# Routing written in another order, later loads in the first mixer, second blocks of 32 slots, one more weight buffer, and products that nothing reads

## The chip, the cores and the metric

One core of a Trainium2 chip runs the whole program in one launch. The metric is the device time of that core in microseconds (us); of several executions the median is taken.

## What is computed

256 tokens of width 1024 pass through two transformer blocks, all in fp32. The reference, cut to what matters here:

```python
# first block
h = x
z = rms_norm(h) @ w_in                       # q, k, v, u: 4 x 512 columns
h = h + concat(diff_attention(q, k, v), pool_mixer(u)) @ w_out
xt = rms_norm(h); logits = xt @ w_router + b_router
top_vals, top_idx = lax.top_k(logits, 4); gates = softmax(top_vals)
# 32 experts: three weights of 1024 x 1024 and three biases each
gt = minimum(x_e @ w_gate[e] + b_gate[e], 7); up = clip(x_e @ w_up[e] + b_up[e], -7, 7)
y_e = ((up + 1) * (gt * sigmoid(1.702 * gt))) @ w_down[e] + b_down[e]
h = h + sum_e gate_e * y_e
h = h + sigmoid(rms_norm(h) @ w_ple_gate) * rms_norm(p @ w_ple_proj)
# second block
x = x + mixer_2(rms_norm(x))                 # sliding window attention and a gated recurrence
x = x + hierarchical_moe(rms_norm(x))        # 4 groups of 8 experts, top 2, 1024 x 512 weights
```

With the reference's inputs the fullest expert of the first mixture gets 73 tokens, the next 64; in the second mixture no expert gets more than 26.

## The kernel before, in words

**Weights.** All large weights stream through SBUF in chunks of 1 MB (`wchunk`, 128 x 2048), which SyncE's queue (SP) loads in the order of use. A chunk goes into the first free buffer of some pools: 7 that stay for the whole kernel, and in the first mixture 4 + 6 more (`NX[False]`, pools `m1_xa` and `m1_xc`). SP takes its loads in order; one that waits for its buffer holds back all loads behind it. The products of the mixers run on split operands (`xh`, `xl` times `w_hi`, `w_lo`): ScalarE (ACT) writes `w_hi`, VectorE (DVE) writes `w_lo`, TensorE (PE) makes three matmuls of 128x512 per piece and token tile. Four such pairs (`AHEAD + 2`) are in flight.

**First mixer** (`attend_pool`, 0 to about 113 us). Four blocks of 512 columns of `w_in` (q, k, v, u), attention as a generator that is advanced between matmuls (`side`), the pool mixer (`bands`, `wpool`), then `w_out`, whose sums are added to the residual `h_res`. Two small tables for what follows are loaded at its start: the experts' biases (`bias_sb`, 786 KB, in two DMAs; ACT copies them, DVE subtracts a low part) and the routers' weights (`wr_sb`, 278 KB; DVE multiplies them by the norm's gains).

**Route** (`route`, once for each mixture). For each of the two token tiles t: turn `h_res` (PE transposes into `ts`, evacuated as `w_hi` by ACT and DVE), `logits`, `choose` (DVE: top k, one-hot `sel`), `keep` (`xth` on ACT, its low part `xtl` in two halves on DVE), `place` (PE products `po` of `sel` with triangular and constant matrices: a token's slot within its expert). `weights` makes the gates and, as int32, the counts `cnt`. Then the one-hots `P`, and the gather (`ga`: PE, 8 matmuls per bank) that brings the tokens of four (second mixture: eight) experts into `xg`. The order on each engine is as written (`manual_schedule`).

**Mixtures.** `all_experts` does 64 slots of an expert with 512 columns at a time: `gate(e+1)`, `down(e)`, `up(e+1)`. If an expert has more than 64 tokens, a second block of 64 slots (`extra`) is done at once, with the same weights still in their buffers. If one has more than the limit of `more` (128), its weights are loaded again. With these inputs the second block is needed once, for expert 0. `narrow_experts` does the second mixture: 32 slots of an expert, four products of 256 columns that lie on the four quarters of PE's rows.

Of the kernel before, what the change touches and what calls it, by code (L numbers as in the profile page):

```python
# [78 lines left out]
class Prog:  # L79
# [346 lines left out]
    def specs(self):  # L426
# [116 lines left out]
    def attend_pool(self, ph, xh, xl):  # L543

        nc, tc = self.nc, self.tc
        if True:
# [7 lines left out]
            wpool = sb.tile([128, 4, 128], F32, name="wpool")  # L554
# [55 lines left out]
            self.wr = self.cst.tile([128, 8, 68], F32, name="wr_sb")  # L610
            nc.sync.dma_start(self.wr, self.A["wr"])
            for g, a, b in ((PK_FFN, 0, 32), (PK_NORM2, 32, 68)):
                col = self.pk[:, g:g + 8].unsqueeze(2).to_broadcast([128, 8, b - a])
                self.tt(self.wr[:, :, a:b], self.wr[:, :, a:b], col, OP.mult)
# [19 lines left out]
            self.cp(self.bias, bias)  # L634
            low = self.bias[64:128]
            self.tt(low, bias[64:128], low, OP.subtract)
# [3 lines left out]
            for _ in side:  # L640
                pass
            return acc
# [153 lines left out]
    def mixer2(self):  # L796
        nc, tc = self.nc, self.tc
        with ExitStack() as ph:
# [7 lines left out]
            with tc.tile_pool(name="b_ple", bufs=2, reuse_waits="tile") as gp:  # L806
                ws = self.p_q
                self.pieces_begin(sp, 29, 0)
                self.norm_tr(self.h[:, 0], 0, xh, xl)
                ss = self.small.tile([128, 2, 2], F32, name="gss")  # L810
# [24 lines left out]
                for t in range(2):  # L835
                    for n in range(4):
                        for i in range(2):
                            self.lin_mm(ps[t], xh, xl, 2 * n + i, ws[n], i, t, n == 0 and i == 0, n == 3 and i == 1)
                        if t == 0 and n == 1:
                            self.norm_tr(self.h[:, 1], 1, xh, xl)  # L840
                            self.piece_emit()
                            stats()
                        if t == 0 and n == 3 or t and n < 2:
                            self.piece_emit()
                    gated(0)(t, ps[t])
# [374 lines left out]
    def route(self, ph, xh, xl, accs):  # L1220
# [17 lines left out]
        def turn(t):  # L1238
            x = r["xT"][t] = self.sp.tile([128, 8, 128], F32, name="w_hi", bufs=self.AHEAD + 2)
            for k4 in range(2):  # L1240
                ps = self.ps.tile([128, 4, 128], F32, name="ts", bufs=3)
                for k in range(4):
                    i = 4 * k4 + k
                    self.tr(ps[:, k], self.h[:, t, i * 128:(i + 1) * 128])
                if k4:
# [4 lines left out]
        def keep(t):  # L1250

# [3 lines left out]
            f = r["r"][:, t:t + 1]  # L1255
            self.cp(xth, xp, f)
            for i in range(2):
                at = (slice(None), slice(None), i) if k == 2 else (slice(None), i)
                self.stt(xtl[at], xp[at], f, xth[at], OP.mult, OP.subtract)
# [4 lines left out]
        def mid():  # L1264
            turn(0)

# [3 lines left out]
        def added(j):  # L1270
            add = self.res(j)

            def f(t, p):
                add(t, p)
                if t == 0:
                    squares(t, j)
                    if j:
                        factor(0)
                        keep(0)
            return f  # L1280

        with tc.manual_schedule():
# [88 lines left out]
    def one_hots(self, c, e0, ne, base, n=64):  # L1371

        P = self.scr.tile([128, 2, ne, n], FR, name="P" if ne > 1 else "PT2", bufs=2 if ne > 1 else 1)
# [4 lines left out]

    def gather(self, c, P):

        ne, n = P.shape[2:]
        xg = self.scr.tile([128, 8, ne, n], F32, name=f"xg{ne}", bufs=1)
        per = 512 // (ne * n)

        def banks():
            for k0 in range(0, 8, per):
                ps = self.bank("ga").rearrange("p (k e s) -> p k e s", k=per, e=ne)
# [15 lines left out]

    def gathered(self, c, P):
        xg, banks = self.gather(c, P)
# [21 lines left out]
    def slots(self, c, e, buf, base=0, n=64):  # L1427
# [6 lines left out]
        i = base // 32 if n == 64 else 8  # L1434
        slot = self.slot[:, i:i + 1]
        self.ts(PT, ps[:, 0], slot, OP.is_equal)
        room = self.scr.tile([128, 2, 128], F32, name="room", bufs=1)
# [20 lines left out]
    def act_fn(self, c, g, u, hd=None, room="act_s"):  # L1458

        nc, scr, W = self.nc, self.scr, c["W"]  # L1460
# [13 lines left out]
        return hd  # L1474

# [58 lines left out]
    def first_tokens(self, c):  # L1534

        P = self.one_hots(c, 0, *((8, 0, 32) if c["second"] else (4, 0)))
        xg, banks = self.gather(c, P)
# [3 lines left out]
    def bias_sel(self, c, e, eng=None):  # L1541
# [3 lines left out]
        sel = self.scr.tile([128, 2, 64], FR, name="bselx" if eng else "bsel", bufs=1 if eng else 2)  # L1545
# [26 lines left out]
    def all_experts(self, c):  # L1572
# [6 lines left out]
        def product(e, part, main, extra):  # L1579
# [3 lines left out]
            with tc.If(st["cnt", e] > 64):  # L1583
                extra(keep)
            self.w_done(4)

        def gate(e, sides=()):
# [4 lines left out]
            def extra(ws):  # L1592
                st["xx"] = self.gathered(c, self.one_hots(c, e, 1, 64))
                gx = self.linear_up(c, st["xx"], 0, ws, sel, self.bias[:, 0], self.bank("ga"))
                hx = st["hx", e] = self.scr.tile([128, c["W"]], F32, name="gx", bufs=2)
                self.cp(hx, gx)
# [3 lines left out]
        def up(e, room="act_s"):  # L1600
# [3 lines left out]
            def extra(ws):  # L1604
                ux = self.linear_up(c, st["xx"], 0, ws, sel, self.bias[:, 1], self.bank("tph"))
                self.act_fn(c, st["hx", e], ux, st["hx", e], room)
# [6 lines left out]
        def down(e, hT, sides):  # L1613
# [3 lines left out]
            def extra(ws):  # L1617
                PTx, gsx = self.slots(c, e, 2, 64)
                yx = self.linear_down(c, self.turn_h(c, st["hx", e], "act_x"), ws, sel, self.bank("ga"))
                for _ in self.combine(c, PTx, self.weigh(yx, gsx, ("act_x", "gxm"))):  # L1620
                    pass
# [6 lines left out]
        for e in range(32):  # L1628
# [7 lines left out]
            if e == 29:  # L1636
                self.w_keep = [self.xps["m1_xa"]] * 4
# [13 lines left out]
            if e == 30:  # L1651
                room = lambda: self.xps["m1_xa"].tile([128, 2048], F32, name="wchunk")
                self.pieces_begin(None, 2, 4, room)
# [111 lines left out]
    def more(self, c):  # L1765

        tc, most = self.tc, 32 if c["second"] else 128
# [52 lines left out]
    NX = {False: (4, 6), True: (4, 5, 3)}  # L1820
# [68 lines left out]
```

## Time and profile before

| what | value |
|---|---|
| three executions | 1806.77, 1803.26 and 1806.77 us |
| profiled execution | 1803.07 us, span in the trace 1801.2 us |
| PE, DVE, ACT busy | 87%, 38%, 21% of the span |
| DMA | 658.88 MB, 366 GB/s in the mean |
| first mixer, first route | 0 to 113 us, 113 to 128 us |
| first mixture | 128 to 1108 us |
| second mixer, second route | 1108 to 1317 us, 1317 to 1348 us |
| second mixture | 1348 to 1797 us |

The profiled execution lies 0.2% below the median, like the second of the three. Starts are in us from the beginning of the span. A busy PE also runs at one of two clocks: a granted clock of 1.0 is 2.4 GHz, 0.5 is 1.2 GHz. What ended an engine's idle time stands in brackets behind a row.

### The profile page before, as it was taken

What the parts mean: (1) busy time and instruction counts of PE and PEld (TensorE: products, weight loads), DVE (VectorE), ACT (ScalarE), POOL (GpSimd) and SP (SyncE); (2) the same over time, 40 slices, a digit from 0 to 9 for tenths busy, and PEclk for the clock granted to TensorE, in tenths of its full rate; (3) what the DMA queues carried; (4) which work ended last, traced back from release to release, by engine and by line L of the source; (5) the groups of instructions that cost most, each with busy time, mean ns of one, the idle gap of its engine ahead of it and who ended that gap; (6) DMA issues with size and microseconds to landing.
All of it is one profiled execution on the core that took longest, in us unless ns stands there. A gap on an engine that the chain in (4) does not pass through costs nothing. (4 is left out here: it accounts for less than half of the span.)

```text
span 1801.2 us, 24529 instructions
## 1 busy us (share of the span) xinstructions
PE 1566.4 (87%) x9887; PEld 763.6 (42%) x9887; DVE 678.2 (38%) x1389; ACT 373.6 (21%) x765; POOL 25.2 (1%) x61
## 2 busy tenths in 40 slices
PE   6989999999998988989899988999979777777776
PEld 5763333333332322323233324789965433433333
DVE  4851222222322222222132334878754333323234
ACT  5631010010100100101001023786632100100100
POOL 0000000000000000000000000000000000000000
PEclk9989999999999999999899999999989977979788
DMA  9374899999999999999999997533669999999997
GB/s 349 125 297 177 328 423 424 422 423 422 424 423 424 423 424 423 423 422 424 421 424 422 424 403 307 191 121 131 242 244 404 423 424 424 424 423 423 421 424 313
DMA packets 109979, 658.88 MB, mean 366 GB/s; under 512 B 10480, under 2 KB 12400, under 8 KB 36080
## 3 DMA queue, kind: packets, MB, share of 16 engines
q1 hardware_dynamic: 108944, 655.19, 89.0%
q8 instruction: 119, 1.95, 0.4%
q10 hardware_dynamic: 720, 0.79, 0.1%
q0 software_dynamic: 144, 0.52, 0.1%
q14 instruction: 52, 0.43, 0.1%
HBM read 655.41 MB, written 1.05 MB: 364 GB/s over the span
## 5 line engine op out<-in xcount | busy, mean ns | idle before, releaser
L94 DVE TENSOR_TENSOR h_res<-h_res,cmb 128x512 f32<-128x512 f32 x260 | 167.1, 684 | 320.4 <-PE cmb L85 320.4
L85 PE MATMUL u<-wchunk,xg 128*64 128x512 f32 x1024 | 236.3, 604 | 21.6 <-DMA wchunk<-in_w_up_dram 21.5
L85 PE MATMUL g<-wchunk,xg 128*64 128x512 f32 x1024 | 250.3, 611 | 0.0
L85 PE MATMUL y<-wchunk,act_s 128*64 128x512 f32 x1024 | 236.7, 600 | 6.1 <-DMA wchunk<-in_w_down_dram 6.1
L85 PE MATMUL gu<-wchunk,xg 128*32 128x256 f32 x2048 | 181.4, 462 | 67.5 <-DMA wchunk<-in_w_up_experts_dram 39.4
L85 PEld LDWEIGHTS u<-wchunk,xg 128*64 128x64 f32 x1024 | 68.4, 138 | 169.3 <-issue 113.7
L85 PEld LDWEIGHTS gu<-wchunk,xg 128*32 128x32 f32 x2048 | 74.8, 128 | 152.4 <-DMA wchunk<-in_w_up_experts_dram 55.4
L85 PEld LDWEIGHTS y<-wchunk,act_s 128*64 128x64 f32 x1024 | 66.7, 136 | 131.1 <-issue 106.5
L91 ACT ACTIVATE yh<-y,gs 128x512 fp32r<-128x512 f32 (+1 forms) x64 | 37.2, 581 | 394.1 <-PEq L1583 286.9
L102 DVE SCALAR_TENSOR_TENSOR yl<-y,gs,yh 128x512 fp32r<-128x512 f32 (+1 forms) x64 | 39.5, 617 | 196.6 <-ACT yh L91 196.5
L85 PEld LDWEIGHTS g<-wchunk,xg 128*64 128x64 f32 x1024 | 62.9, 137 | 106.5 <-issue 95.3
L85 PE MATMUL cmb<-yh,PT 32*128 32x256 f32 (+1 forms) x384 | 75.4, 460 | 31.6 <-DVE h_res L94 30.5
L91 ACT ACTIVATE act_s<-tph 128x256 f32<-128x256 f32 x32 | 12.3, 384 | 361.5 <-PE tph L88 361.5
L85 PE MATMUL lin<-w_hi,xh 128*128 128x512 f32 (+1 forms) x192 | 77.8, 405 | 10.4 <-ACT w_hi L91 8.9
L102 DVE SCALAR_TENSOR_TENSOR w_lo<-wchunk,pk_sb,w_hi 128x512 fp32r<-128x512 f32 (+1 forms) x120 | 83.3, 729 | 9.0 <-ACT w_hi L91 8.6
L85 PEld LDWEIGHTS cmb<-yh,PT 32*128 32x128 f32 (+1 forms) x384 | 33.1, 203 | 117.5 <-DVE h_res L94 64.5
L91 ACT ACTIVATE w_hi<-wchunk,pk_sb 128x512 fp32r<-128x512 f32 (+1 forms) x120 | 77.9, 699 | 16.7 <-PE lin L85 14.1
L98 DVE TENSOR_SCALAR act_h<-u 128x512 f32<-128x512 f32 x32 | 22.1, 692 | 156.3 <-PE u L85 156.3
L85 PE MATMUL lin<-w_lo,xh 128*128 128x512 f32 (+1 forms) x192 | 75.6, 394 | 5.6 <-DVE w_lo L102 4.7
L98 DVE TENSOR_SCALAR PT<-ga,cmain 128x256 fp32r<-128x256 f32 x65 | 31.0, 477 | 121.1 <-PE ga L85 121.1
L85 PE MATMUL lin<-w_hi,xl 128*128 128x512 f32 (+1 forms) x192 | 75.5, 393 | 0.5 <-DVE xl L125 0.5
L85 PE MATMUL y<-wchunk,hT 128*32 128x256 f32 x1024 | 65.0, 385 | 10.4 <-DMA wchunk<-in_w_down_experts_dram 9.7
(386 smaller groups left out, 1923.0 us busy)
## 6 DMA issues: line engine op xcount, KB each, us to landing
wchunk<-in_w_gate_dram SPq DMA_DIRECT2D x128, 1024.0 KB, 19.7
wchunk<-in_w_up_dram SPq DMA_DIRECT2D x128, 1024.0 KB, 19.7
wchunk<-in_w_down_dram SPq DMA_DIRECT2D x128, 1024.0 KB, 19.7
wchunk<-in_w_gate_experts_dram SPq DMA_DIRECT2D x64, 1024.0 KB, 19.7
wchunk<-in_w_up_experts_dram SPq DMA_DIRECT2D x64, 1024.0 KB, 19.7
wchunk<-in_w_down_experts_dram SPq DMA_DIRECT2D x64, 1024.0 KB, 19.7
wchunk<-in_w_in_dram SPq DMA_DIRECT2D x27, 1024.0 KB, 5.4
wchunk<-in_w_out_dram SPq DMA_DIRECT2D x8, 1024.0 KB, 5.1
```

Source lines behind the costliest of these rows:

```text
L85: self.nc.tensor.matmul(out, lhsT, rhs, start=start, stop=stop, skip_group_check=True)
L91: self.nc.scalar.activation(out=out, in_=in_, func=AF.Copy, scale=scale)
L94: self.nc.vector.tensor_tensor(out=out, in0=a, in1=b, op=op)
L98: (eng or self.nc.vector).tensor_scalar(out=out, in0=a, scalar1=s1, scalar2=s2, op0=op0, **kw)
L102: self.nc.vector.scalar_tensor_tensor(out=out, in0=a, scalar=s, in1=b, op0=op0, op1=op1, **kw)
```

## The change

- **First mixer.** The loads of the biases and the routers' weights, and the ACT and DVE work on them, go from the mixer's start to its end. They share the room of `bands` and `wpool`, so they wait until the pool mixer's matmuls have read these. The work on them is written behind the attention's last step.
- **Route.** The squares of tile 1 go into the evacuation of its sums, its norm factor ahead of the first choice, and its `xth`/`xtl` behind the second choice; one half of `xtl` is left until the one-hots are there. For tile 1 both evacuations of the turned residual are ACT's. PE gets 11 matmuls of 128x512 between the two `place`, and 5 behind the second, whose result nothing reads (`busy`).
- **Second block.** 32 slots (65 to 96) in place of 64: four products of 256 columns on quarters of PE's rows (`quarters`), as in the second mixture. The limit of `more` goes from 128 to 96.
- **Buffers.** `m1_xc` has 7 (18 in all); the one-hots of the first mixture lose one of two buffers.
- **`w_ple_gate`.** One of its chunks goes behind the first mixture's last `down` chunk; it was split before that mixture's end, and now at the second mixer's start.

```diff
@@ the order of the weights
-                    cols(A["w_ple_gate"][0], 0, 512, PK_PLE)
+                    cols(A["w_ple_gate"][0, 0:512], 0, 512, PK_PLE)
...
         mixture(False)
+        cols(A["w_ple_gate"][0, 512:1024], 0, 512, PK_PLE + 4)
@@ attend_pool
-            bias = sb.tile([128, 3, 512], F32, name="bias_sb")
-            for r in range(2):
-                nc.sync.dma_start(bias[64 * r:64 * r + 64], self.A["bias"].rearrange("(j r) n -> r j n", j=3))
...
-            self.wr = self.cst.tile([128, 8, 68], F32, name="wr_sb")
-            nc.sync.dma_start(self.wr, self.A["wr"])
...
+            bias = sb.tile([128, 4, 384], F32, name="bands").rearrange("p a n -> p (a n)")
...
+            wr = sb.tile([128, 8, 68], F32, name="wpool")
+            nc.sync.dma_start(wr, self.A["wr"])
             acc = [self.lin_banks() for j in range(2)]
             for j in range(2):
                 self.lin_acc(acc[j], mh, ml, 4, 4, True, False, side)
             for _ in side:
                 pass
+            tc.keep_in_program_order(nc.scalar.activation(out=flat, in_=bias, func=AF.Copy))
+            tc.keep_in_program_order(nc.vector.tensor_tensor(out=low, in0=bias[64:128], in1=low, op=OP.subtract))
...
@@ route
+        def busy(n):
+            ps = self.ps.tile([128, 512], F32, name="ts", bufs=3)
+            for _ in range(n):
+                self.mm(ps, self.onesr, xh[:, 0:2].rearrange("p k t -> p (k t)"), True, True)
...
             turn(1)
+            factor(1)
             self.choose(c, r, 0)
-            for j in range(2 - len(accs), 2):
-                squares(1, j)
-            factor(1)
-            keep(1)
             self.logits(c, r, 1)
             self.place(r, 0, pp)
             self.choose(c, r, 1)
+            busy(11)
             self.place(r, 1, pp)
+            busy(5)
+            keep_high(1)
+            keep_low(1, 0)
+            c["rest"] = lambda: keep_low(1, 1)
             self.weights(c, r, pp)
@@ the second block
+    def quarters(self, c, x, ws, sel, part, ps):
...
+        for w in ws:
+            for j in range(w.shape[1]):
+                lhs = x[:, k, 0] if part < 2 else x[:, j, q4[k // 2]]
+                for q, o in enumerate(q4):
+                    self.mm(ps[o], lhs, w[:, j, 256 * q:256 * q + 256], False, k == 7)
+                k += 1
@@ more, buffers
-        tc, most = self.tc, 32 if c["second"] else 128
+        tc, most = self.tc, 32 if c["second"] else 96
-    NX = {False: (4, 6), True: (4, 5, 3)}
+    NX = {False: (4, 7), True: (4, 5, 3)}
```

SP's queue from the last chunks of `w_in` to the first mixture's first chunks, before:

```order
L154 DMA wchunk<-in_w_in_dram 128x4x512 x6
L154 DMA wchunk<-in_w_out_dram 128x4x512
L551 DMA aux<-in_cst_dram 128x512
L553 DMA bands<-in_bands_dram 128x1536
L555 DMA wpool<-in_w_pool_dram 128x4x128
L560 DMA bias_sb<-in_bias_dram 64x3x512 x2
L154 DMA wchunk<-in_w_out_dram 128x4x512
L611 DMA wr_sb<-in_wr_dram 128x544
L616 DMA pf<-in_p_dram 128x2x256
L154 DMA wchunk<-in_w_out_dram 128x4x512 x2
L154 DMA wchunk<-in_w_gate_dram 128x2048 x4
L154 DMA wchunk<-in_w_up_dram 128x2048 x4
```

and now:

```order
L154 DMA wchunk<-in_w_in_dram 128x4x512 x6
L154 DMA wchunk<-in_w_out_dram 128x4x512
L552 DMA aux<-in_cst_dram 128x512
L554 DMA bands<-in_bands_dram 128x1536
L557 DMA wpool<-in_w_pool_dram 128x4x128
L154 DMA wchunk<-in_w_out_dram 128x4x512
L609 DMA pf<-in_p_dram 128x2x256
L154 DMA wchunk<-in_w_out_dram 128x4x512 x2
L154 DMA wchunk<-in_w_gate_dram 128x2048 x4
L630 DMA bands<-in_bias_dram 64x3x512 x2
L632 DMA wpool<-in_wr_dram 128x544
L154 DMA wchunk<-in_w_up_dram 128x2048 x2
```

Three loads moved from the front of the queue to behind the first four expert chunks.

DVE from the mixer's last `xl` to the first choice (`le` begins a choice, `sel` ends it), before:

```order
L102 SCALAR_TENSOR_TENSOR xl<-ts,subln_404,xh 128x4x128
L94 TENSOR_TENSOR h_res<-h_res,lin 128x512
L94 TENSOR_TENSOR rr<-rss 128x1
L98 TENSOR_SCALAR rr<-rr 128x1
L102 SCALAR_TENSOR_TENSOR xtl<-h_res,rr,xth 128x4x128 x2
L94 TENSOR_TENSOR h_res<-h_res,lin 128x512
L1246 COPY w_hi<-ts 128x512
L94 TENSOR_TENSOR h_res<-h_res,lin 128x512
L1246 COPY w_hi<-ts 128x512
L102 SCALAR_TENSOR_TENSOR le<-lin,rr,rw_sb 128x32
```

and now:

```order
L102 SCALAR_TENSOR_TENSOR xl<-ts,subln_401,xh 128x4x128
L642 TENSOR_TENSOR bias<-bands,bias 64x1536
L645 TENSOR_TENSOR wr_sb<-wpool,pk_sb 128x8x32
L645 TENSOR_TENSOR wr_sb<-wpool,pk_sb 128x8x36
L94 TENSOR_TENSOR h_res<-h_res,lin 128x512
L94 TENSOR_TENSOR rr<-rss 128x1
L98 TENSOR_SCALAR rr<-rr 128x1
L102 SCALAR_TENSOR_TENSOR xtl<-h_res,rr,xth 128x4x128 x2
L94 TENSOR_TENSOR h_res<-h_res,lin 128x512
L1254 COPY w_hi<-ts 128x512
L94 TENSOR_TENSOR h_res<-h_res,lin 128x512
L94 TENSOR_TENSOR rr<-rss 128x1
```

The work on the tables now stands ahead of the second addition to `h_res`, and the factor of tile 1 ahead of the choice of tile 0.

PE from the logits of tile 1 to the first gather in the changed kernel (before, the same rows without the two of `ts<-xh,onesr`):

```order
L85 MATMUL lin<-wr_sb,w_hi 128x32 x8
L85 MATMUL po<-sel,trir 128x32
L85 MATMUL po<-sel,onesr 128x32 x2
L85 MATMUL ts<-xh,onesr 128x512 x11
L85 MATMUL po<-sel,trir 128x32
L85 MATMUL po<-sel,onesr 128x32
L85 MATMUL ts<-xh,onesr 128x512 x5
L85 MATMUL ga<-P,xth 128x256
```

Eleven matmuls now stand ahead of the second `place` and five behind it.

## Rows read from the trace of the kernel before

**Rows 1.** The page's chain that ended last, shares of the span by engine.

```profile
DMA 23%; PE 10%; DVE 3%; ACT 2%; issue 1%; DVEq 0%; SPq 0%; ACTq 0%
```

**Rows 2.** Windows: stretch, length, busy us of each engine, clock, DMA share, GB/s.

```profile
36.00:52.00 16.00, 4.97 (x12) 3.35 (x11) 7.25 (x11) 6.95 (x10) 0.00 (x0) 0.58 0.63 186
118.00:134.00 16.00, 9.90 (x44) 7.20 (x45) 7.66 (x32) 5.01 (x15) 1.51 (x4) 0.57 0.90 351
136.00:148.00 12.00, 11.53 (x71) 6.60 (x69) 0.69 (x1) 1.50 (x4) 0.00 (x0) 1.00 0.00 0
149.00:221.00 72.00, 67.29 (x296) 22.52 (x294) 17.59 (x32) 6.71 (x12) 0.40 (x1) 0.98 0.77 293
221.00:1100.00 879.00, 809.52 (x3607) 274.21 (x3603) 231.86 (x415) 83.72 (x163) 12.33 (x30) 0.99 1.01 421
...
1338.00:1352.00 14.00, 5.17 (x26) 4.34 (x30) 6.80 (x29) 4.71 (x14) 0.89 (x3) 0.53 0.18 64
...
1357.00:1790.00 433.00, 324.30 (x3730) 162.08 (x3722) 156.96 (x351) 51.07 (x123) 0.00 (x0) 0.86 1.00 420
```

**Rows 3.** Timeline of PE in the first mixer: start, us, instructions, idle before.

```profile
35.95 0.39 PE L85 MATMUL lin<-w_hi,xl 128*128 128x512 f32 x1
43.98 0.79 PE L85 MATMUL lin<-w_hi,xh 128*128 128x512 f32 x1 [7.63 <-ACT w_hi L91]
48.17 0.79 PE L85 MATMUL lin<-w_lo,xh 128*128 128x512 f32 x1 [3.40 <-DVE w_lo L102]
```

**Rows 4.** Timeline of ACT and DVE in the same stretch.

```profile
41.83 1.48 ACT L91 ACTIVATE bias<-bias_sb 128x1536 fp32r<-128x1536 f32 x1 [12.49 <-DMA bias_sb<-in_bias_dram]
44.69 0.43 DVE L94 TENSOR_TENSOR wr_sb<-wr_sb,pk_sb 128x256 f32<-128x256 f32 x1 [12.87 <-DMA wr_sb<-in_wr_dram]
45.58 1.76 DVE L94 TENSOR_TENSOR bias<-bias_sb,bias 64x1536 fp32r<-64x1536 f32 x1
```

**Rows 5.** Timeline of DVE where the mixer ends.

```profile
108.61 0.69 DVE L94 TENSOR_TENSOR h_res<-h_res,lin 128x512 f32<-128x512 f32 x1 [0.84 <-PE lin L85]
```

**Rows 6.** Timeline of DVE and PE, first route and first gather.

```profile
123.20 0.24 DVE L102 SCALAR_TENSOR_TENSOR le<-lin,rr,rw_sb 128x32 f32<-128x32 f32 x1
124.96 0.40 PE L85 MATMUL po<-sel,trir 128*128 128x32 f32 x1 [4.53 <-DVE sel L1329]
126.44 0.55 PE L85 MATMUL ga<-P,xth 128*128 128x256 f32 x1 [0.87 <-DVE s L1362]
131.43 3.21 PE L85 MATMUL g<-wchunk,xg 128*64 128x512 f32 x8
135.71 1.94 PE L85 MATMUL g<-wchunk,xg 128*64 128x512 f32 x8
```

**Rows 7.** Timeline of PE: a second block's product, an expert's in the second mixture.

```profile
163.13 7.09 PE L85 MATMUL tph<-wchunk,xg 128*64 128x512 f32 x32
1358.47 3.66 PE L85 MATMUL gu<-wchunk,xg 128*32 128x256 f32 x64
```

**Rows 8.** Timeline of ACT and PE near the first mixture's end.

```profile
1070.24 2.56 ACT L91 ACTIVATE wchunk<-wchunk,pk_sb 128x512 fp32r<-128x512 f32 x4 [1.11 <-DMA wchunk<-in_w_ple_gate_dram]
1072.71 5.75 PE L85 MATMUL u<-wchunk,xg 128*64 128x512 f32 x18 [5.02 <-DMA wchunk<-in_w_up_dram]
```

**Rows 9.** Timeline of DVE, PE and SP in the second route.

```profile
1334.43 1.98 PE L85 MATMUL lin<-wr_sb,w_hi 128*128 128x36 f32 x16 [0.25 <-ACT w_hi L91]
1342.37 0.22 DVE L102 SCALAR_TENSOR_TENSOR l<-lin,rr,rw_sb 128x4 f32<-128x4 f32 x1
1345.04 0.40 PE L85 MATMUL po<-sel,trir 128*128 128x32 f32 x1 [7.06 <-DVE sel L1329]
1346.51 0.55 PE L85 MATMUL ga<-P,xth 128*128 128x256 f32 x1 [0.87 <-DVE P L94]
1348.30 0.33 SPq L154 DMA_DIRECT2D wchunk<-in_w_up_experts_dram  x1
...
1355.24 0.33 SPq L154 DMA_DIRECT2D wchunk<-in_w_up_experts_dram  x1
```

More of the change, by code (lines that the diff above doesn't have):

```diff
@@ L807, in mixer2 @@
                 ws = self.p_q
-                self.pieces_begin(sp, 29, 0)
+                self.pieces_begin(sp, 30, 0)
                 self.norm_tr(self.h[:, 0], 0, xh, xl)
+                for _ in range(2):
+                    self.piece_emit()
+                    ws.append(self.piece(False))
                 ss = self.small.tile([128, 2, 2], F32, name="gss")
@@ L1250, in keep, with parts @@
         def keep(t):
+            keep_high(t)
+            for i in range(2):
+                keep_low(t, i)
+        def parts(t):
             k = 2048 // c["ff"]
@@ L1254, in keep, with keep_high, keep_low @@
             xth, xtl = (c[n][:, t].rearrange("p (c k q) -> p c k q", k=k, q=128) for n in ("xth", "xtl"))
-            f = r["r"][:, t:t + 1]
+            return k, xp, xth, xtl, r["r"][:, t:t + 1]
+        def keep_high(t):
+            k, xp, xth, xtl, f = parts(t)
             self.cp(xth, xp, f)
-            for i in range(2):
-                at = (slice(None), slice(None), i) if k == 2 else (slice(None), i)
-                self.stt(xtl[at], xp[at], f, xth[at], OP.mult, OP.subtract)
+        def keep_low(t, i):
+            k, xp, xth, xtl, f = parts(t)
+            at = (slice(None), slice(None), i) if k == 2 else (slice(None), i)
+            self.stt(xtl[at], xp[at], f, xth[at], OP.mult, OP.subtract)
         def factor(t):
@@ L1274, in f @@
                 add(t, p)
[L1275 to L1279, printed above, removed]
+                squares(t, j)
+                if t == 0 and j:
+                    factor(0)
+                    keep(0)
             return f
@@ L1371, in one_hots @@
     def one_hots(self, c, e0, ne, base, n=64):
-        P = self.scr.tile([128, 2, ne, n], FR, name="P" if ne > 1 else "PT2", bufs=2 if ne > 1 else 1)
+        P = self.scr.tile([128, 2, ne, n], FR, name="P" if ne > 1 else "PT2", bufs=2 if c["second"] and ne > 1 else 1)
         for t in range(2):
@@ L1377, in one_hots, with gather @@
         return P
-    def gather(self, c, P):
+    def gather(self, c, P, name=None):
         ne, n = P.shape[2:]
-        xg = self.scr.tile([128, 8, ne, n], F32, name=f"xg{ne}", bufs=1)
-        per = 512 // (ne * n)
+        if ne == 1 and not (name or c["second"]):
+            name = "P"
+        xg = self.scr.tile([128, 8, ne, n], F32, name=name or f"xg{ne}", bufs=1)
+        per = min(8, 512 // (ne * n))
         def banks():
             for k0 in range(0, 8, per):
-                ps = self.bank("ga").rearrange("p (k e s) -> p k e s", k=per, e=ne)
+                ps = self.bank("ga")[:, :per * ne * n].rearrange("p (k e s) -> p k e s", k=per, e=ne)
                 for i in range(per):
@@ L1402, in gather, with gathered @@
         return xg, banks()
-    def gathered(self, c, P):
-        xg, banks = self.gather(c, P)
+    def gathered(self, c, P, name=None):
+        xg, banks = self.gather(c, P, name)
         for _ in banks:
@@ L1544, in bias_sel @@
             return None
-        sel = self.scr.tile([128, 2, 64], FR, name="bselx" if eng else "bsel", bufs=1 if eng else 2)
+        sel = self.scr.tile([128, 2, 64], FR, name="pg" if eng else "bsel", bufs=1 if eng else 2)
         col = lambda n: self.identr[:, n:n + 33:32].unsqueeze(2).to_broadcast([128, 2, 64])
@@ L1590, in gate, with extra @@
             g = st["g"] = self.bank("g")
[L1592 to L1596, printed above, removed]
+            def extra(ws, base):
+                st["xx"] = self.gathered(c, self.one_hots(c, e, 1, base, 32), "xg32")
+                st["hx", e] = self.scr.tile([128, 256], F32, name="gx", bufs=2)
+                self.cp(st["hx", e], self.quarters(c, st["xx"], ws, sel, 0, self.bank("ga")))
             product(e, 0, lambda ws: self.linear_up(c, xg, e % 4, ws, sel, self.bias[:, 0], g,
@@ L1602, in up, with extra @@
             u = self.bank("u")
[L1604 to L1606 removed]
+            def extra(ws, base):
+                ux = self.quarters(c, st["xx"], ws, sel, 1, self.bank("tph"))
+                hx = st["hx", e]
+                self.act_fn(c, hx, ux, hx, room)
             def main(ws):
```

72 lines of the change are left out of this document (50 added, 22 removed).

## The prediction

> **What bounds the kernel now.** I read the chain that ended last first [rows 1]: 23% of the span hangs on DMA and 10% on PE, so there are stretches of two kinds. The windows tell them apart [rows 2]. From 221 to 1100 us and from 1357 to 1790 us the DMA engines are busy all the time (share 1.01 and 1.00, 420 GB/s): there the weights' stream is the bound, one chunk of 1.049 MB each 1.049/0.421 = 2.49 us, and a faster engine gains nothing. Elsewhere the stream waits for buffers, that is for PE: its share is 0.00 from 136 to 148 us and 0.77 from 149 to 221 us, while PE is busy for 11.53 of 12 and 67.29 of 72 us. What is saved ahead of a saturated stretch brings its start forward, and with it everything behind, as long as the stream still has idle time to give up: 12 us and 0.23 x 72 = 16.6 us here. Then I read the timelines of the stretches that the change touches, and ask in each what ends PE's wait last. A warm matmul of 128x512 takes 7.09/32 = 0.222 us [rows 7]; the profiled execution took 1803.07 us, and the terms below are set against that.
>
> **The first mixer: -13.3 us.** After the matmul at 35.95 us PE waits 7.63 us for `w_hi`, makes one matmul, and waits 3.40 us for `w_lo` [rows 3]. Both waits have the same kind of cause [rows 4]: ACT stood 12.49 us at the copy of the biases, whose load had not landed, with the next `w_hi` behind it in its order; DVE stood 12.87 us at the product on the routers' weights, then did 0.43, about as much again and 1.76 us on both tables before the next `w_lo`. Meanwhile the granted clock fell, so that the next matmuls ran at half rate: 12 of them in the 16 us from 36 to 52 us at a clock of 0.58 [rows 2]. At full clock 12 take 2.7 us; that leaves 13.3 us. In the new order neither the three loads nor the work stands there. Bounds: nothing else late gives up the whole; if the next piece of `w_in` or its splitting were late by a third, some 9 us remain. I take 13.3.
>
> **The tables' work at its new place: +2.4 us.** It stands ahead of the second addition to `h_res`, on which the norm, the turn and the logits of tile 0 wait. DVE has 0.84 us of idle time before that addition [rows 5]; the work there is 0.43 + about 0.43 + 1.76 = 2.6 us [rows 4], and it also needs ACT's copy of 1.48 us first, of which perhaps 0.6 us shows behind the `xl` before it. 2.6 + 0.6 - 0.84 = 2.4; bounds 1.8 (copy hidden) and 4.1 (nothing hidden). The loads themselves stand in SP's queue behind the gate chunks and ahead of the up chunks, so these wait with them until the pool mixer's matmuls are through; their products come only after those of the first gate, and I take nothing for it.
>
> **The first route: -1.9 us.** Before, the second choice came after `xth` and `xtl` of tile 1; from its start to `place` it took 124.96 - 123.20 = 1.76 us, and PE had waited 4.53 us [rows 6]. The new order drops 1.3 us of `xtl` and overlaps 1.2 us of `xth`: about -2.5 us for `sel`. Against it, ACT's squares of tile 1 now stand ahead of its evacuation of tile 0, which delays the logits by some 0.8 us; the second `place` waits until the 11 products are through (2.4 us from the first `place`, about 1.2 us longer than `sel` needs); and here the one-hots `P` come behind the counts, some 1.6 us of small DVE work. So the gather begins about 1.2 us later than by the tables' work alone. What comes back is the clock: it was 0.57 from 118 to 134 us [rows 2]. The first product of eight matmuls took 3.21 us, the next 1.94; the two cold banks of the gather with a bias product between took 131.43 - 126.44 = 4.99 us, while a warm one fits between 134.64 and 135.71, 1.1 us [rows 6]. Warm, the two would take about 3.1 us. 1.3 + 1.8 = 3.1 us back, so 1.2 - 3.1 = -1.9. If the clock has fallen before the 11 products begin, they take 4.9 us in place of 2.4, and the sum is about +1; if it isn't back by the gather either, +4.
>
> **The second block: -10.6 us.** It runs once, in three parts, each 7.09 us for 32 matmuls. The nearest row for the new form is an expert of the second mixture, the same products on quarters: 3.66 us [rows 7]. 3 x 3.43 = 10.3 us, and 0.3 for evacuations of half the width. All three lie ahead of 221 us, where PE is the bound and the stream waits for what it frees [rows 2]. Bounds: 8 (the additions to `h_res` become eight small ones in place of four) and 11.5.
>
> **The 18th buffer: -2.4 us.** One chunk more is loaded in the idle stretch from 136 to 148 us; the saturated stretch has one less to bring. Bounds 0 and 2.5.
>
> **The moved chunk: -2 us.** The first mixture ends with the stream (PE waits 5.02 us for an `up` chunk [rows 8]), and one chunk less before its last `down` gives 2.49 us. Splitting it moves into the second mixer's start, 2.56 us of ACT work [rows 8] beside PE's products; I take 0.5 of it. Bounds +0.1 and -2.5.
>
> **The second route: -5.1 us.** The logits end at 1334.43 + 1.98 = 1336.4 us; the choice from its start to `place` took 1345.04 - 1342.37 = 2.67 us, after PE had waited 7.06 us [rows 9]. In the new order it starts at 1336.4 and ends at 1339.1. The 11 products start after the first `place`, at 1337.0, and end at 1339.4, so `place` comes some 5.6 us earlier. Here the one-hots directly follow it; the gather would start about 5 us earlier and warm, where the clock was 0.53 [rows 2]. The stream stood still until 1348.30 us, when the counts were written, and again until 1355.24 us, when the first chunk was free [rows 9]. The counts have half of `xtl`, 1.1 us, put ahead of them: -4.4 us. The second wait, which ends with PE's first products, shrinks as the gather gets 5 us earlier and warm, by some 2 us at most. I take -5.1; bounds -2 (cold products, 2.4 us later) and -6.5.
>
> Sum: -13.3 + 2.4 - 1.9 - 10.6 - 2.4 - 2.0 - 5.1 = -32.9, so 1770.2 us for an execution like the profiled one. Two of three runs shown lie 3.7 us above it; for a median I put **1772 us**.
>
> **Rivals.**
> *The clock.* The products come too late to hold it: in the first route PE now waits about 3 us more ahead of the logits, since the tables' work delays them, and the clock fell where PE idled for 7.63, 4.53 and 7.06 us [rows 3, 6, 9]. Then both routes pay for the products and save little: +4 and -2 in place of -1.9 and -5.1, that is 9 us less gain, 1781 us. The Trainium skill ("TensorE: Matmul & The Clock Gate", Part 1: The HAM clock gate) says that the throttled state is the default and that activity releases it. By it the products would either hold the clock or, if it has fallen, win it back ahead of the gather at the price of their own slow run. The trace agrees as to the two levels, 1.00 and 0.50.
> *The mixer's wait is only exchanged.* With the biases gone, the piece after 36 us could wait for another load that stood in the same queue. The wait's releasers are ACT and DVE, not a chunk's DMA, which speaks against it. If half of the stretch stays, 6.7 us less gain: 1778.5 us.
> *The stream hides it.* If the saturated stretch began when it does for a reason other than PE, all that is saved ahead of 221 us would be lost, and only the moved chunk and the second route count: -7.1 us, 1799.5 us at the median. The idle shares of 1.00 and 0.23 before it [rows 2] speak against that.
> *Slower.* The limit of `more` is now 96. Should an expert have more than 96 tokens, its 12 chunks are loaded a second time; one after another at the stream's pace that is 12 x 2.49 = 30 us, but each load waits until its products free the one buffer, and a load that nothing overlaps costs several times that. From a price of 33 us on the kernel is slower; at 90 us it would take 1862 us. It decides from the 97th token of one expert; with these inputs the fullest has 73.
> *No change.* This needs the mixer's gain and the second block's both lost, and one route slower.
>
> **How the numbers follow.** My forecast, all terms near their values: 0.60. The clock: 0.16. The mixer's wait exchanged: 0.11. The stream: 0.08. Slower: 0.03. No change: 0.02. With each term at its better bound the median would be some 1762 us, a little less if the runs are like the profiled one; with the worse bounds of routes, mixer and second block together some 1786. The range 1759 to 1788 holds the first three cases, 0.87 in all, and leaves some of their edges; the forecast's own is 1765 to 1778. Some 0.2%, 3.6 us, is what a measurement of this kernel tells from no change: faster 0.95, same 0.02, slower 0.03.
>
> **What would show it.** In the new profile: PE without a stall between 36 and 40 us, and the first route some 11 us earlier; DVE's work on the tables ahead of the second addition to `h_res`, with that much idle time on PE after it; a granted clock near 1.0 from the first gather on; `cmb`, `g` and `u` of the second block as rows of 64 matmuls in about 3.7 us; the stream saturated from some 197 us on and again from about 1320 us; the last `down` chunk of the first mixture followed by three chunks of `w_ple_gate`. The prediction is wrong if the mixer's stall has another releaser, if a saturated stretch keeps its start although PE is earlier, or if a clock of 0.5 covers both gathers.

## The result, and the profile after

The changed kernel took 1777.21 us in the median of four runs (1776.37 to 1778.57), before 1806.53 us (1803.26 to 1806.77): a ratio of 0.9841, 95% interval 0.9826 to 0.9856, 29 us less. The profiled execution took 1776.37 us, 26.7 us less than the one profiled before. The forecast was 1772 us, the range 1759 to 1788.

Two executions of one kernel differ by up to 3.5 us here and by 4.6 us in two of the experiments; so I follow one pair of profiles and read at which places a start moved, and by how much:

| place (read in both traces) | before | after | moved by | gained or lost there |
|---|---|---|---|---|
| first `w_hi`, `xh` product of the first mixer | 10.28 | 9.75 | -0.5 | -0.5 |
| last `xl` of the first mixer | 107.02 | 91.66 | -15.4 | -14.9 |
| second addition to `h_res` [rows 5] | 108.61 | 95.52 | -13.1 | +2.3 |
| end of the first gate product | 134.64 | 122.78 | -11.9 | +1.2 |
| 13th `down` chunk landed | 252.96 | 229.10 | -23.9 | -12.0 |
| 121st `down` chunk landed | 1082.55 | 1061.34 | -21.2 | +2.7, with one chunk less |
| 13th chunk of the second `w_in` issued | 1166.55 | 1144.83 | -21.7 | -0.5 |
| end of the execution | 1803.07 | 1776.37 | -26.7 | -5.0 |

The stall in the first mixer is gone. The windows of PE after (length, busy us of PE, PEld, DVE, ACT and POOL, clock, DMA share, GB/s), to be held against the first of [rows 2]:

```profile
36.00:52.00 16.00, 16.00 (x79) 12.61 (x78) 15.23 (x34) 10.40 (x24) 0.19 (x1) 1.00 0.76 293
```

79 matmuls in 16 us at a clock of 1.00, where 12 had been made. DVE's timeline where the mixer now ends, to be held against [rows 5]:

```profile
91.66 0.75 DVE L102 SCALAR_TENSOR_TENSOR xl<-ts,subln,xh 128x512 fp32r<-128x512 f32 x1 [0.88 <-ACT xh L91]
93.04 1.75 DVE L642 TENSOR_TENSOR bias<-bands,bias 64x1536 fp32r<-64x1536 f32 x1 [0.63 <-ACT bias L641]
94.81 0.80 DVE L645 TENSOR_TENSOR wr_sb<-wpool,pk_sb 128x256 f32<-128x256 f32 x2
95.52 0.68 DVE L94 TENSOR_TENSOR h_res<-h_res,lin 128x512 f32<-128x512 f32 x1
```

DVE waits 0.63 us for ACT's copy, then works 2.5 us on the tables: the addition comes 3.1 us after `xl` is done, where it came 0.84 us after it. In the first route, PE's timeline (to be held against [rows 6]) shows what follows:

```profile
102.61 2.63 PE L85 MATMUL lin<-wr_sb,w_hi 128*128 128x32 f32 x16 [3.06 <-ACT w_hi L91]
105.05 1.95 PE L88 MATMUL ts<-cmain,h_res 128*128 128x128 f32 x8
106.83 3.62 PE L85 MATMUL lin<-wr_sb,w_hi 128*128 128x32 f32 x16
...
110.91 4.20 PE L85 MATMUL ts<-xh,onesr 128*128 128x512 f32 x11
114.95 0.18 PE L85 MATMUL po<-sel,trir 128*128 128x32 f32 x1
...
117.58 0.38 PE L85 MATMUL ga<-P,xth 128*128 128x256 f32 x1 [1.08 <-DVE P L94]
...
120.84 1.94 PE L85 MATMUL g<-wchunk,xg 128*64 128x512 f32 x8
```

and the windows beside it:

```profile
100.00:104.00 4.00, 1.39 (x12) 1.40 (x12) 2.82 (x6) 1.93 (x5) 0.17 (x1) 0.96 0.87 369
104.00:114.00 10.00, 10.00 (x40) 9.13 (x41) 3.84 (x16) 3.27 (x9) 0.00 (x0) 0.50 0.24 79
114.00:123.00 9.00, 7.41 (x39) 4.78 (x38) 3.35 (x13) 1.78 (x6) 1.19 (x4) 1.00 1.01 427
```

PE waits 3.06 us for the logits' operand, the clock falls behind that wait, and from 104 to 114 us all runs at half rate, the 11 products too: 4.20 us. They bring the clock back (without them it was still 0.50 from 116 to 120 us, see "no products"); gather and gate product are warm (1.94 us in place of 3.21). The second block's first product ran at half rate for a part of its time, the two others did not (PE's timeline):

```profile
134.71 5.19 PE L85 MATMUL ga<-wchunk,xg 128*32 128x256 f32 x64
...
148.94 3.64 PE L85 MATMUL tph<-wchunk,xg 128*32 128x256 f32 x64
...
170.90 3.66 PE L85 MATMUL ga<-wchunk,act_x 128*32 128x256 f32 x64 [0.56 <-DVE act_x L1668]
```

What I had not looked for is in the list of DMA queues of the saturated stretch, 230 to 1050 us (packets, MB, share of 16 engines). Before:

```profile
q1 hardware_dynamic: 47666, 345.67, 100.6%
q8 instruction: 62, 1.02, 0.5%
```

After:

```profile
q1 hardware_dynamic: 47751, 343.50, 100.4%
q8 instruction: 88, 1.44, 0.7%
```

26 fetches of instructions more, 16 KB each, and 2.2 MB of weights less in the same 820 us. Where chunks land every 2.48 us, some come about 1.2 us late (I count from 0.9 us on): 7 times in this stretch before, 11 times after. Between one late chunk and the next lie exactly eight of these packets, in both profiles, and a late chunk lands 2 to 4 us behind the last of them. The late chunks add up to 8.7 us before and 12.6 us after. At all seven late chunks before and at ten of the eleven after, eight loads are under way, the usual number there, so it is not SP that waits for a buffer.

In the second route the 11 products ran mostly at half rate in this execution (PE's timeline, to be held against [rows 9]):

```profile
1314.81 0.28 PE L85 MATMUL po<-sel,trir 128*128 128x32 f32 x1
...
1315.16 4.36 PE L85 MATMUL ts<-xh,onesr 128*128 128x512 f32 x11
1319.36 0.18 PE L85 MATMUL po<-sel,trir 128*128 128x32 f32 x1
...
1324.22 1.07 PE L85 MATMUL gu<-wchunk,xg 128*32 128x256 f32 x16
```

The stream's second standstill there, between a first chunk of `w_gate_experts` and the next of `w_up_experts`, is shorter than in [rows 9] (SP's timeline):

```profile
1323.73 0.42 SPq L154 DMA_DIRECT2D wchunk<-in_w_gate_experts_dram  x1
1327.46 0.33 SPq L154 DMA_DIRECT2D wchunk<-in_w_up_experts_dram  x1
```

### The profile page after: what moved, and what is told of

Its sections match the earlier page's. It is cut to its first block, busy times and chain, and to the rows that moved or that the text cites. A ratio compares the mean times of both kernels' runs of the same rounds, so it can differ in the third digit from the quotient of the medians.

```text
span 1774.6 us, 24791 instructions
## 1 busy us (share of the span) xinstructions
PE 1559.6 (88%) x10042; PEld 766.9 (43%) x10042; DVE 675.7 (38%) x1391; ACT 373.8 (21%) x766; POOL 26.3 (1%) x61
## 5 line engine op out<-in xcount | busy, mean ns | idle before, releaser
L94 DVE TENSOR_TENSOR h_res<-h_res,cmb 128x512 f32<-128x512 f32 (+1 forms) x260 | 166.0, 680 | 326.3 <-PE cmb L85 313.6
```

The lines of the kernel that those rows point to most:

```text
L94: self.nc.vector.tensor_tensor(out=out, in0=a, in1=b, op=op)
```

## The experiments

Every ratio is to the kernel before, run beside it on the same chip (1806.2 to 1807.6 us); 1777.2 us is the changed kernel's own median. Four runs each unless said otherwise. The chips differ: the kernel before has medians 1.4 us apart on them. So a difference of less than some 3 us between two medians tells nothing by itself, and there I go by the traces.

**Later loads alone.** The kernel before with `attend_pool` of the changed one.

> The kernel before with one part of the change: the loads of the biases and the routers' weights and the work on them at the mixer's end. My theory: PE no longer stops at 36 us, which gave 15.4 us in the changed kernel; the work at its new place delays the second addition to h_res by 2.3 us; the route is the old one, with the clock down in its gather as before. All of it lies ahead of the saturated stretch and carries: 1806.5 - 13.1 = about 1793.4 us. Rival, the stream hides it: the saturated stretch begins as before, 1803 to 1807 us. Rival, the gain needs the new route: between 1797 and 1800 us.

Measured 1795.12 us, ratio 0.9931 (0.9914 to 0.9948): 12.5 us less. My theory holds; the stream does not hide it, and it needs no new route.

**The tables' work at another place.** In the changed kernel:

```diff
-            for j in range(2):
-                self.lin_acc(acc[j], mh, ml, 4, 4, True, False, side)
-            for _ in side:
-                pass
...
+            self.lin_acc(acc[0], mh, ml, 4, 4, True, False, side)
             tc.keep_in_program_order(nc.scalar.activation(out=flat, in_=bias, func=AF.Copy))
             tc.keep_in_program_order(nc.vector.tensor_tensor(out=low, in0=bias[64:128], in1=low, op=OP.subtract))
+            self.lin_acc(acc[1], mh, ml, 4, 4, True, False, side)
...
+            for _ in side:
+                pass
```

> The changed kernel with the copy and subtraction of the biases between the two halves of the products on w_out, where DVE is idle for 2.2 us, and the product on the routers' weights ahead of the attention's last step. My theory: the second addition to h_res comes some 2.3 us earlier, PE's wait ahead of the logits shrinks from 3.06 to about 0.8 us, so the clock does not fall there, logits, turn and products run at full rate, and the first gate product ends 4 to 5 us earlier: 1772 to 1773 us. Rival, the clock falls in the route anyway (it did so in the kernel before, with no such wait): only 2.3 us, about 1775 us. Rival, the work now delays the splitting of w_out instead: no gain, 1777 us.

Measured 1772.26 us, 0.9803 (0.9787 to 0.9819): 5 us less than the changed kernel. But only half of my theory holds. PE's timeline in the first route:

```profile
100.29 2.07 PE L85 MATMUL lin<-wr_sb,w_hi 128*128 128x32 f32 x16 [0.65 <-ACT w_hi L91]
...
103.95 3.62 PE L85 MATMUL lin<-wr_sb,w_hi 128*128 128x32 f32 x16
...
108.03 4.73 PE L85 MATMUL ts<-xh,onesr 128*128 128x512 f32 x11
```

The wait shrank from 3.06 to 0.65 us, and the clock fell all the same, as the rival said; the gate product began 2.4 us earlier, what the tables' work had cost. At the second mixer's 13th chunk that was still 2.4 us (1142.48 for 1144.83), at the second route's `place` 3.9 us (1315.43 for 1319.36): the 11 products took 2.81 us there this time and not 4.36, without any edit near. The profiles end 3.3 us apart, the medians 5. One profile does not settle when the clock falls: the kernel with one second block beside the stream (below) has the same route, and there the clock was 0.84 from 104 to 108 us and 0.74 from 108 to 112, where it was 0.50 here, and the second `place` came 2.9 us earlier (109.73 for 112.59).

**No products.** Both calls of `busy` removed from the changed kernel.

> The changed kernel without the 11 and the 5 products that nothing reads. My theory: in the first route the second place follows its choice at once, 2.3 us earlier, but the clock, which fell ahead of the logits, does not come back before the gather: two banks and the first gate product cost 3.1 us more, so +0.8; in the second route place is at most 0.5 us earlier and gather and first products are cold, +2.5. In all about 1780 us. Rival, the products only delay place and the clock comes back in the gather as fast: 1774 to 1775 us. Rival, no difference: 1777 us.

Measured 1777.82 us, 0.9838 (0.9822 to 0.9855): no difference that this measures. The first route did lose what I expected, 1.0 us at the end of the first gate product (123.80 for 122.78; the clock was 0.50 from 116 to 120 us, with the products 1.00), but the stream took no harm: the 13th `down` chunk landed at 228.75 us, with the products at 229.10. In the second route the products brought next to nothing in these two profiles: from the mixer's last addition but one to `h_res` to the first product of the experts it took 21.2 us without them (1304.20 to 1325.43) and 21.1 us with them (1303.14 to 1324.22). I had priced the loss there too high.

**More products, earlier.** In the first route of the changed kernel:

```diff
             pp = self.ps.tile([128, 3, 32], F32, name="po", bufs=1)
+            if not c["second"]:
+                busy(12)
             self.logits(c, r, 0)
```

> The changed kernel with 12 more products that nothing reads (2.7 us at full rate) in the first route ahead of the first logits, where PE waits 3.06 us for them; the other 11 and 5 stay. My theory: it is this wait that lets the clock fall; without it the first turn, logits and the 11 products run at full rate, some 0.9 + 1.6 + 1.7 us less, and the first gate product ends about 4 us earlier: 1773 us. Rival, the clock falls anyway among the short products of logits and turn: 1777 us, or up to 1779 us if the added products also delay the logits.

Measured 1772.76 us, 0.9806 (0.9789 to 0.9822), 4.5 us less. Here the clock does hold through the route up to `place` (PE's timeline):

```profile
99.44 2.95 PE L85 MATMUL ts<-xh,onesr 128*128 128x512 f32 x12
102.64 1.97 PE L85 MATMUL lin<-wr_sb,w_hi 128*128 128x32 f32 x16 [0.25 <-ACT w_hi L91]
...
105.76 1.97 PE L85 MATMUL lin<-wr_sb,w_hi 128*128 128x32 f32 x16 [0.25 <-ACT w_hi L91]
...
107.91 2.81 PE L85 MATMUL ts<-xh,onesr 128*128 128x512 f32 x11
110.56 0.18 PE L85 MATMUL po<-sel,trir 128*128 128x32 f32 x1
...
113.80 0.39 PE L85 MATMUL ga<-P,xth 128*128 128x256 f32 x1 [1.69 <-DVE P L94]
```

`place` comes 4.4 us earlier than in the changed kernel, the gather 3.8 us. Then the clock fell once more (0.59 from 116 to 120 us), and the first gate product ended 2.2 us earlier (120.62 for 122.78); the 13th `down` chunk landed 3.5 us earlier. So what the products bring hangs on where they stand: the half-rate stretch costs `place` over 4 us, and products behind it run at half rate themselves.

**Code for one second block.** The second block written for expert 0 alone; with these inputs no other expert needs one, and for other inputs this kernel would leave out tokens:

```diff
-            with tc.If(st["cnt", e] > 64):
-                extra(keep, 64)
+            if e == 0:
+                with tc.If(st["cnt", e] > 64):
+                    extra(keep, 64)
```

> The changed kernel with the code of the second block written for expert 0 alone; the other 31 experts have no second block at all (with these inputs none of them needs one). What is executed in the second block is the same. My theory: the 6.3 us that the changed kernel lost between 230 and 1057 us, in stalls of the weights' stream of 1.1 to 1.2 us at regular distances, are paid for PE's instructions being fetched: the narrow second block's code, which is jumped over 31 times, makes the program longer. Without it the stalls are rarer than in the kernel before (7 there, 11 now, 1 to 4 here) and the time falls by 8 to 12 us: 1766 to 1769 us. Rival, the stalls come at regular times for another reason (memory refresh, the profiler): same number, 1776 to 1778 us.

Measured 1761.24 us, 0.9748 (0.9732 to 0.9764): 16 us less than the changed kernel, more than I expected. The list of queues, 230 to 1050 us:

```profile
q1 hardware_dynamic: 48238, 347.05, 101.0%
q8 instruction: 29, 0.48, 0.2%
```

29 fetches in place of 88, 3.55 MB more weights in the same time, and no chunk late by 0.9 us or more. From the 13th to the 121st `down` chunk it took 819.8 us, in the changed kernel 832.2. That is 12.4 of the 17.9 us by which the two profiles differ.

Another 4.5 us lie ahead of the 13th chunk, behind a first gate product that ended at the same time (122.86 for 122.78), and they have other causes. 1.5 us is the clock: the block's first product took 3.66 us here and 5.19 there. The other 3 us are pauses of PE at the branches, which are written for the first expert alone here. The largest is the one behind an `up` product (PE's timeline of the changed kernel):

```profile
188.21 0.47 PE L85 MATMUL g<-bias,bsel 128*128 128x512 f32 x1 [1.01 <-DVE act_h L98]
```

In this run the same matmul (185.42 us) follows without a wait. The kernel before, with shorter code behind its branches, has that pause too (1.02 us at 209.39), so the change did not bring it.

**More code that never runs.** The kernel before, with a branch that no count takes:

```diff
             self.w_done(4)
+            with tc.If(st["cnt", e] > 200):
+                ps = self.bank("ga")
+                for _ in range(48):
+                    self.mm(ps[:, 0:128], self.onesr, self.onesr, True, True)
```

> The kernel before with 48 more matmuls behind each of the first mixture's 96 products, in a branch that no count of these inputs takes: some 5000 PE instructions that are never executed, about as many as the change added. My theory: fetching them costs the weights' stream what the longer program costs the changed kernel; about 85 to 90 fetches of 16 KB in place of 62 between 230 and 1050 us, 10 stalls in place of 7, +4 to +6 us: 1811 to 1813 us. Rival, code that is jumped over isn't fetched and the cause lies in the narrow block itself: 1807 us.

Measured 1818.24 us, 1.0070 (1.0053 to 1.0087): 12 us more, twice what I expected, for instructions that are not executed. 94 fetches and 12 late chunks in the stretch:

```profile
q1 hardware_dynamic: 47303, 343.04, 100.2%
q8 instruction: 94, 1.54, 0.8%
```

From the 13th to the 121st `down` chunk it took 836.7 us, before 829.6: 7.1 us lie in the saturated stretch. The two profiles end 15.4 us apart. Of the rest, 2.5 us lie ahead of the end of the first gate product, where none of the added code stands yet, 3.4 us between there and the 13th `down` chunk, and 2.5 us behind the 121st. This run adds 96 branches together with their code and does not tell the one from the other; the next one does.

**The wide second block.** The changed kernel with the second block of before and 17 buffers.

> The changed kernel with the second block of before (64 slots, two products of 512 columns) and 17 buffers in place of 18. My theory: three products of 7.1 in place of 5.2, 3.6 and 3.7 us, 8.7 us, and one chunk less ahead, 2.1 us, so 1777 + 11; and the stream gets back what the longer code costs, 3 to 6 us: about 1783 us. Rival, the block's length is hidden behind the stream: 1774 us or less. Rival, the code costs nothing: 1788 us.

Measured 1788.47 us, 0.9897 (0.9880 to 0.9913), against 1781.04 us for the next one, which differs in the block alone: 7.4 us. Its three products took 8.78, 7.09 and 7.09 us, 10.3 us more than the narrow ones there (5.35, 3.64 and 3.66); the instruction queue fetched 63 times in the stretch and not 88, and the way from the 13th to the 121st `down` chunk took 826.6 us, 5.4 less. Both kernels have the same branches, so these 5.4 us are the price of longer code alone. From the first gate product to the 13th `down` chunk the narrow block gains 11.3 us, and it gives half of that back in fetches. The time is the one that the rival gave for code that costs nothing, but not for its reason: the first product ran partly at half rate here too, and the first gate product ended 1.8 us later than with 17 buffers alone (126.05 for 124.28), ahead of all that differs.

**17 buffers.** `NX = {False: (4, 6), ...}` in the changed kernel.

> The changed kernel with 17 buffers in place of 18. My theory: one chunk less is loaded while PE works on expert 0, so the saturated stretch has one more to bring: +2.1 to +2.5 us, 1779.5 us. Rival, the stream has no idle time left there: 1777 us.

Measured 1781.04 us, 0.9850 (0.9834 to 0.9867): 3.8 us more, or 2.9 if each is held against the kernel before on its own chip; from the first gate product to the 13th `down` chunk 2.8 us more, about the chunk that I expected. The rest lies within what executions differ by.

**The moved chunk back.** The chunk of `w_ple_gate` again ahead of the last expert's.

> The changed kernel with the chunk of the gate of the embedding back ahead of the last expert's chunks and split there, as before. My theory: the last down chunk lands 2.5 to 3.7 us later and the second mixer starts that much later, less some 0.5 us of splitting: 1779.5 to 1780.5 us. Rival, the split at the mixer's start costs what the chunk saves: 1777 us.

Measured 1778.28 us, 0.9843 (0.9827 to 0.9860): inconclusive by time. In the trace the last `down` chunk landed 2.5 us later (1082.52 for 1080.03) and the second route began 2.8 us later, as my theory has it; then its 11 products ran at full rate, `place` was only 1.2 us later than in the changed kernel's profile, and the last chunk 0.6 us. The clock in the second route hid most of the difference.

**64 columns in the second block's gather** (17 buffers, one run).

> The changed kernel with 17 buffers and 64 columns in place of 32 in the second block's gather, of which 32 are used; to be read against the run with 17 buffers. My theory: it is the gather's 64 matmuls of 32 columns that let the clock fall, so that the block's first product took 5.2 us at half rate; with 64 columns it keeps 1.00 and takes 3.7 us. The gather itself keeps its length. Rival, the clock falls there anyway: 5.2 us again.

Measured 1779.59 us. The rival was right: the block's first product took 5.17 us again. The number of columns in the gather is not what lets the clock fall there; what is, stays open. The gather alone does not decide it: in "code for one second block" and in the two kernels that follow here, the same product behind the same gather of 32 columns took 3.66 us.

**One second block beside the stream, for all inputs.** Expert 0 as in the changed kernel; any other expert with more than 64 tokens goes to `more`, whose limit for them is 64; the biases' work between the halves of `w_out`.

```diff
-        tc, most = self.tc, 32 if c["second"] else 96
...
+        first = 0 if c["second"] else 1
+        if first:
+            blocks(0, 96)
+        most = 64 if first else 32
         with tc.If(self.count(c, 32, (ET.Pool,)) > most):
...
+            for e in range(first, 32):
+                blocks(e, most)
```

> The changed kernel with the biases' work between the halves of w_out, and with a second block beside the stream for expert 0 alone; all other experts with more than 64 tokens go to the blocks that load their weights again (limit 64 in place of 96; the largest count is taken over experts 1 to 31). Nothing is left out for other inputs. My theory: both gains add, -5 and -16 us from 1777.2: 1756 to 1758 us. Rival, the shorter program's gain was partly the earlier start of a stretch that ends in another bound: 1760 us or more.

Measured **1755.67 us**, 0.9727 (0.9710 to 0.9743): 21.5 us less than the changed kernel, the fastest here. It has a price: with other inputs, each expert beyond the first that overflows loads its weights again.

> The same without the products that nothing reads. My theory after their removal from the changed kernel gave no difference: they cost in the first route by delaying place what they give by the clock, and in the second route give about 1 us: 1757 to 1759 us, 0 to 2 us more than with them. Rival, they are worth 3 us, as predicted from the cold gathers: 1760 us.

Measured 1758.55 us, 0.9743 (0.9727 to 0.9759): the products bring 2.9 us here, with intervals that just overlap; in the changed kernel they brought 0.6. I leave it at 0 to 3 us as they stand. In the traces 2.7 us of it lie in the first route (first gate product at 117.71 and 120.41 us).

## Why the prediction was right, and where it was off

- **The first mixer, -13.3 forecast.** Right in place and mechanism: -14.9 between the first product and the last `xl`, and "later loads alone" shows it by itself. I closed the account at 52 us, where the clock was back, but of PE's products on `w_in` the 101st had gained 12.5 us (49.61 for 36.60, less the start's 0.5), the 121st 13.7 and the 151st all 14.9 (67.41 for 52.01). The 1.6 us beyond the forecast are within what executions differ by: in the profile of "later loads alone" the gain at the same place is 13.3 us.
- **The tables' work, +2.4.** Measured +2.3, by the DVE rows.
- **The first route, -1.9.** Measured +1.2; the step that failed is "what comes back is the clock". I let the products hold the clock and named as a rival that the tables' delay would let it fall first. It did fall first: the clock was at 0.50 from 104 to 114 us, the products took 4.2 us in place of 2.4, and +1 was the sum that the prediction gave for that case. But the delay is not the whole cause, as I had made it: with a wait of 0.65 us the clock fell as well. With products ahead of the logits it held up to `place`, in the one profile that there is. Nor do the 1.2 us come from the new order. In the profile of "later loads alone", with the old route, it took 27.4 us from the second addition to the end of the first gate product; in the changed kernel it took 27.3 us, before 26.0 us. So the loss came with the tables' work, and the new order and its products together gave nothing there.
- **The second block and the 18th buffer, -10.6 and -2.4.** Together -12.0. The block's three products took 12.5 us where three times 3.66 was forecast, since the first ran partly at half rate. The buffer is one chunk, by the experiment.
- **The moved chunk, -2.0.** One chunk at the first mixture's end and -0.5 us at the second mixer's start, in which the split took ACT 2.55 us and held up nobody: -3.0. The 0.5 us say little, since the same stretch took 82.7 to 85.0 us in the profiles of the other kernels that have this order, and 83.5 here.
- **The second route, -5.1.** Measured -5.0 to the end of the execution, although the products ran at half rate for the most part; my bound for that was -2. The second standstill of the stream shrank from 6.6 to 3.7 us, by more than the 2 us that I had allowed. In these profiles the gain is that of the order, hardly of the products: from the mixer's last addition but one to the first product of the experts it took 26.7 us before and in "later loads alone", 21.1 us in the changed kernel, 21.2 without the products, and 19.6 where the 11 products ran at full rate.
- **What was missing.** No term of the sum, no rival held the fetch of instructions: the new code in branches that are not taken was put at nothing, without a reason. In the saturated stretch the changed kernel needs 832.2 us where before needed 829.6 less one chunk, 827.1: 5.1 us lost, of which the late chunks make 4.0. "Code for one second block" and "more code" show from both sides that such code with its branches costs time, and "the wide second block" that its length alone does. This is the largest error of the prediction, hidden by the two terms that came out better.

The sum for an execution like the profiled one was 1770.2 us, the profiled one took 1776.4: 6.2 us more. 5.1 of them are fetches, 3.1 the first route and 1.0 the second block, less 2.1 up to the mixer's end and 1.0 at the moved chunk. That the time lies so near the forecast is thus in part luck. Two of the prediction's smaller sums are off, too: the better bounds that it states add up to 3.5 us, which gives some 1768 us and not 1762, and 6.7 us less gain is 1778.7 us and not 1778.5.

## What to carry to other kernels

When two engines stand in order behind loads for something that is needed much later, move the loads and the work, and give the work a place where its engine idles: the move gave 12.5 us, the place some 2.4 more. Where the weights' stream is the bound, unrolled code has a price even if it is jumped over; count the instruction queue's packets in the saturated stretch before and after an edit. Where PE is the bound, the branch itself can have one: look for waits of PE behind it. Products that only keep PE busy brought 4.5 us by the medians where they stood ahead of the first idle time, and 0 to 3 us behind it, where they ran at half rate and held up what came after.

## What the runs showed of the hardware

- **Fetches of instructions.** 62, 88, 94, 63 and 29 packets of 16 KB in 820 us (before, changed, more code, wide block, one block's code); chunks late by 0.9 to 1.3 us: 7, 11, 12, 6 and 0. In the first four, exactly eight packets lie between each late chunk and the next. With one block's code the longest delay is 0.8 us. Each packet takes about 1.06 us of one DMA queue's time in the mean, by the packets' own records. Why it is every eighth, no run shows. The Trainium skill ("Runtime: NRT & Kernel Launch", Instruction fetch mechanics) says that instructions are refilled in blocks of 16 KiB ahead of execution and that the cost is mostly hidden. The size agrees (1.44 MB / 88 = 16.4 KB); hidden it is not where the weights' stream keeps the DMA engines busy all the time.
- **The clock in the routes.** The same 11 products in the second route took 2.81 us in four kernels' profiles and 4.27 to 4.36 us in five others', with no edit near. 1.5 us of a comparison between two of these kernels can be that.
